# Second feed-forward layer: tiles 4 to 20 as seven products of half blocks instead of eight

## The chip, the cores and the metric

The kernel runs on one core of a Trainium2 chip. The time is device microseconds of one execution; the kernel before was timed three times, and a further execution was recorded by the hardware profiler. The engines in the profile are PE (matrix products; PEld loads its stationary operand), DVE (VectorE), ACT (ScalarE), POOL (GpSimd) and SP (SyncE, which issues nearly all transfers). Each engine works through one queue of instructions in a fixed order, and waits on semaphores for what other engines produce.

## The reference

Two decoder layers on 512 positions of width 1024, in f32: a mixer (gated linear attention in layer 0, latent attention in layer 1), then a feed-forward block. Only the feed-forward block of layer 1 is changed:

```python
def swiglu(h, w_in, w_out):
    gate, up = jnp.split(h @ w_in, 2, axis=-1)
    return (jax.nn.silu(gate) * up) @ w_out
...
        h = modulate(x, norm_ffn[i], sh2, sc2)
        x = x + g2[:, None, :] * swiglu(h, ffn_w_in[i], ffn_w_out[i])
```

`w_in` is 1024 x 5632 (gate and up, 2816 columns each), `w_out` is 2816 x 1024. The 2816 inner columns are 22 tiles of 128.

## The kernel before

Activations are kept transposed: 128 features on the partitions, 512 positions along the free axis. `h` is eight such k-tiles. Every f32 operand of a product is split into a high part (a cast to fp32r on ScalarE) and a low part (the difference, on VectorE), and every product is three matmuls: high x high, high x low, low x high (`mm3`, L175 to L180).

A weight comes as a **unit**, a block of up to 128 x 1024 (`wunit`, L155 to L173): a load from memory into a buffer `raw` (L158, issued by SP), the cast to `wh` (L164, ScalarE), the low part `wl` (L172, VectorE). `raw`, `wh` and `wl` have three buffers each (pool `wp`), so that a load waits until the low part of the unit three loads back is done.

The first two inner tiles are computed in `boundary`, together with the norm ahead of the block, as 256-wide products `fg` (`group`). Tiles 2 to 21 each take two units (gate and up, 512 KB) and `proj` of 8 k-tiles by 3 matmuls of 512 columns for each; then `glu` takes silu (ScalarE), multiplies (VectorE) and splits the result into `acth` and `actl`.

The **output projection** goes over chunks of tiles, so that finished ones can be consumed: after tile 7 over tiles 0 to 7, after tile 14 over 8 to 14, and over 15 to 21 at the end, in the last `boundary`/`finish`. For each of the 8 output k-tiles, `out_proj` (L307) loads one unit of `nk` x 128 columns, multiplies, and adds the product to the residual `x` on VectorE (L290):

```python
        for n in range(KD):
            w = wunit(src[n], nk * P)
            ps = bank("op")
            proj(ps, w, rhs)
            residual(ps, n, l, j, None)
```

The order of the instructions on each engine is set by a scheduler, except on PE inside `manual_schedule`, where the written order holds. Product banks (PSUM) come from two pools of four, `bank` and `abank`; scratch tiles of 128 x 512 come from a ring (`R`).

Of the kernel before, what the change touches and what calls it, by code (L numbers as in the profile page):

```python
# [9 lines left out]
F32 = mybir.dt.float32  # L10
F32R = mybir.dt.float32r
# [3 lines left out]
ALU = mybir.AluOpType  # L15
# [22 lines left out]

DFF = 2816
NFF = DFF // P  # L40
FF_CHUNKS = ((0, 8), (8, 15), (15, 22))

LEVELS = (1, 2, 4, 8, 16, 32, 64)
QB = 32
# [39 lines left out]
def trunk(ctx: ExitStack, tc: tile.TileContext, t: dict, out: bass.AP):  # L84
# [11 lines left out]
    def R(name, dt=F32, cols=S):  # L96
        return ring.tile([P, cols], dt, tag="ring", name=name, bufs=NRING)

    def bank(name):
        return psm.tile([P, S], F32, tag="mm", name=name)  # L100
# [71 lines left out]
        ins = nc.vector.tensor_tensor(out=wl[:, :n], in0=raw[:, :n], in1=wh[:, :n].bitcast(F32), op=ALU.subtract)  # L172
        last["w"] = ins.ins  # L173

    def mm3(ps, a, b, start, stop):  # L175

        (ah, al), (bh, bl) = a, b
        nc.tensor.matmul(ps, lhsT=ah, rhs=bh, start=start, stop=False)  # L178
        nc.tensor.matmul(ps, lhsT=ah, rhs=bl, start=False, stop=False)  # L179
        nc.tensor.matmul(ps, lhsT=al, rhs=bh, start=False, stop=stop)  # L180

    def sl(pair, *idx):
        return pair[0][idx], pair[1][idx]
# [86 lines left out]
                nc.scalar.activation(out=self.acc[:, c], in_=src, func=AF.Square)  # L270
                self.begun |= set(range(c.start, c.stop, P))

    def modulated(hk, k, l, j, rstd, c=FULL):

        hi, lo = hk
        u = R("u")
        nc.vector.scalar_tensor_tensor(out=u[:, c], in0=x[k][:, c], scalar=gs_t[l][j][:, k:k + 1], in1=rstd[:, c],  # L277
                                       op0=ALU.mult, op1=ALU.mult)
        sh = mod[l][3 * j][:, k:k + 1]
        nc.scalar.activation(out=hi[:, c], in_=u[:, c], func=AF.Identity, bias=sh)  # L280
        ins = nc.vector.scalar_tensor_tensor(out=lo[:, c], in0=u[:, c], scalar=sh, in1=hi[:, c].bitcast(F32),
                                             op0=ALU.add, op1=ALU.subtract)
        last["m"] = ins.ins

    def h_tiles():
        return [(R("hh", F32R), R("hl", F32R)) for _ in range(KD)]
# [25 lines left out]
            proj(ps, w, rhs)  # L312
            residual(ps, n, l, j, None)

    def boundary(src, rhs, l, j, nk, name, also=None, grp=None, gl_=None, gj=None, take=None):

        ss = SumSq()
        A, B = HALVES  # L320
        nf = KD - NH
        gw = []
        for n in range(nf):
# [19 lines left out]
        h = h_tiles()  # L343

        def half(n, c):

            ps = bank("op") if c is A else abank("op")
            proj(ps, ws[n - nf], rhs, c=c)
            residual(ps, n, l, j, ss, c)

        def group(c, ps, ks):
            for k in ks:
                if (c.start, k) not in done:
                    modulated(h[k], k, gl_, gj, rstd, c)
                if c.start and k == 3:
                    last["half"] = last["m"]
                for i in range(4):
                    mm3(ps[i][:, c], sl(gw[k], slice(None), slice(i * P, (i + 1) * P)), sl(h[k], slice(None), c),
                        k == 0, k == KD - 1)

        done = set()
        with tc.manual_schedule(engines={mybir.EngineType.PE}):
            for n in range(nf, KD):
                half(n, A)
            half(nf, B)
            ya = rstd_stats(ss.acc, D, name, A)
            half(nf + 1, B)
            rstd_spread(ya, rstd, name, A)
            with tc.high_priority():
                for k in range(2):  # L370
                    modulated(h[k], k, gl_, gj, rstd, A)
# [12 lines left out]
            take(B, pb)  # L384
        return h
# [505 lines left out]
    def ffn(l, prev):  # L891
# [15 lines left out]
            glu(0, ps[0], ps[1], c)  # L907
            glu(1, ps[2], ps[3], c)

        h = prev(grp=t["ffn_s"][l * 4:(l + 1) * 4], gl_=l, gj=1, take=take)  # L910
        for ci, (a, b) in enumerate(FF_CHUNKS):
            for i in range(max(a, 2), b):
                pr = []
                for gu in range(2):
                    with tc.issue_after(last["half"]):
                        w = wunit(t["ffn_in"][l * 40 + (i - 2) * 2 + gu])
                    ps = bank("f")
                    proj(ps, w, h)
                    pr.append(ps)
                ins = glu(i, *pr)  # L920
                if l == 0:
                    with tc.issue_after(ins.ins):
                        more_ada(3)
            src, rhs = t[f"ffn_o{ci}"][l * KD:(l + 1) * KD], [act[i] for i in range(a, b)]
            if l == 0 and ci == 1:
                with tc.issue_after(ins.ins):
                    rotary()
            if ci < 2:
                out_proj(src, rhs, l, 1, nk=b - a)
        return lambda **kw: boundary(src, rhs, l, 1, b - a, f"nf{l}", **kw)  # L930

    nxt = ffn(0, lambda **kw: boundary(t["gla_wo"], oh, 0, 0, KD, "nm0", also=also, **kw))

# [236 lines left out]
def _pack(inp):  # L1170
# [71 lines left out]

    fi = f("ffn_w_in")
    fo = f("ffn_w_out")
    s_, u_, o_ = [], [], [[], [], []]
    for l in range(2):
        g_, up = fi[l][:, :DFF], fi[l][:, DFF:]
        s_.append(pairs(np.concatenate([g_[:, :P], up[:, :P], g_[:, P:2 * P], up[:, P:2 * P]], axis=1)))
        both = np.stack([outer(g_), outer(up)], axis=1)[2:]
        u_.append(both.reshape(40, P, D))  # L1250
        for ci, (a, b) in enumerate(FF_CHUNKS):
            o_[ci].append(outer(fo[l][a * P:b * P]))
    d["ffn_s"] = np.concatenate(s_)
    d["ffn_in"] = np.concatenate(u_)
    for ci in range(3):
        d[f"ffn_o{ci}"] = np.concatenate(o_[ci])

    mw = f("mla_w_in")[0]
    cq, ckv, kr = np.split(mw, [QR, QR + KVR], axis=1)
# [34 lines left out]
```

## Time and profile before

| what | value |
|---|---|
| median of 3 runs | 1181.49 us (1181.05 to 1186.13) |
| profiled execution | 1182.71 us, span 1180.9 us, mean granted clock 0.993 |
| PE busy | 1157.6 us (98%), 7070 instructions |
| VectorE, ScalarE busy | 724.2 us (61%), 417.0 us (35%) |
| second feed-forward layer, tiles 2 to 21 and two projections | 830.90 to 1130.13 us |
| last projection and final norm | 1130.13 to 1180.9 us |

The page's first part gives each engine's busy time and share of the span. Its fourth part follows the chain of work that ended last back from the end; the shares there say which engine set the time. The table of stretches gives, for a window of the span, each engine's busy time with the number of its instructions, then the granted PE clock (1.00 is full), the busy share of the transfer engines, and GB/s. A row of the timeline gives start, duration, engine, line, operation, output and inputs, and in brackets how long the engine had been idle and what ended that. Matmul ends are modelled: the pace of PE is read from the distance of starts.

### The profile page before, as it was taken

The page shows a single profiled execution, that of the slowest core. Times are in us where ns is not written, and L with a number is a line of the kernel's source. Part 1 is how long each engine was busy: PE and PEld are TensorE (multiplying, and loading weights), DVE is VectorE, ACT ScalarE, POOL GpSimd, SP SyncE. Part 2 cuts the span into 40 slices and gives each one's busy share as a digit, 9 for nine tenths or more (in the row PEclk, how much of TensorE's full clock was granted, in tenths as well). Part 3 has the DMA queues.
Part 4 walks back from the last instruction along what each step waited for, and adds up shares of the span by engine and source line. Part 5 has one row for each costly group of instructions (what it writes and reads, how often), then busy time and mean ns, then how long its engine had stood idle before and what let it go on. Part 6 is the DMA issues. An engine that isn't in the chain of part 4 may idle for free.

```text
span 1180.9 us, 17487 instructions
## 1 busy us (share of the span) xinstructions
PE 1157.6 (98%) x7070; PEld 977.4 (83%) x7070; DVE 724.2 (61%) x1428; ACT 417.0 (35%) x666; POOL 18.1 (2%) x40
## 2 busy tenths in 40 slices
PE   8999999999999999999999899999999999999996
PEld 4877878898888888888899788889888888888886
DVE  6987888875663567657566878757324333333345
ACT  3372445342221222222344456534222132222331
POOL 0000000000000000000000022000000000000000
PEclk9999999999999999999999999999999999999998
DMA  9761264714773577366521124140333323233222
GB/s 347 243 188 65 75 230 126 224 62 126 234 246 107 162 242 247 110 204 226 159 85 48 60 81 108 53 126 14 96 106 90 104 93 90 90 107 106 83 78 72
DMA packets 47378, 156.91 MB, mean 133 GB/s; under 512 B 5601, under 2 KB 8033, under 8 KB 47298
## 3 DMA queue, kind: packets, MB, share of 16 engines
q1 hardware_dynamic: 44322, 152.43, 40.5%
q0 software_dynamic: 1536, 2.10, 0.8%
q10 hardware_dynamic: 1440, 1.28, 0.3%
q8 instruction: 55, 0.90, 0.3%
q14 instruction: 25, 0.20, 0.1%
HBM read 151.59 MB, written 2.10 MB: 130 GB/s over the span
## 4 chain that ended last, share of the span: by engine, by line
PE 90%; DVE 7%; DMA 2%; ACT 1%; issue 1%; POOL 0%; SPq 0%; DVEq 0%; ACTq 0%
PE f L179 12%; PE f L178 12%; PE f L180 12%; PE op L178 9%; PE op L179 9%; PE op L180 9%; PE fg L179 2%; PE fg L178 2%; PE fg L180 2%; DMA adaw<-in_ada 1%; PE r L178 1%; PE r L179 1%; PE r L180 1%; PE v L178 1%; DVE wl L172 1%; PE ko L179 1%
## 5 line engine op out<-in xcount | busy, mean ns | idle before, releaser
L164 ACT CAST wh<-raw 128x1024 fp32r<-128x1024 f32 (+2 forms) x173 | 177.4, 1026 | 553.1 <-PE f L179 179.1
L172 DVE TENSOR_TENSOR wl<-raw,wh 128x1024 fp32r<-128x1024 f32 (+2 forms) x181 | 215.2, 1190 | 107.7 <-ACT wh L164 102.0
L179 PE MATMUL f<-hl,wh 128*128 128x512 f32 x640 | 249.1, 389 | 0.0
L178 PE MATMUL f<-hh,wh 128*128 128x512 f32 x640 | 249.1, 389 | 0.0
L180 PE MATMUL f<-hh,wl 128*128 128x512 f32 x640 | 249.0, 389 | 0.0
L178 PE MATMUL op<-acth,wh 128*128 128x512 f32 (+1 forms) x394 | 144.7, 367 | 0.0
L179 PE MATMUL op<-actl,wh 128*128 128x512 f32 (+1 forms) x394 | 144.4, 366 | 0.0
L180 PE MATMUL op<-acth,wl 128*128 128x512 f32 (+1 forms) x394 | 144.4, 366 | 0.0
L180 PEld LDWEIGHTS f<-hh,wl 128*128 128x128 f32 x640 | 120.1, 188 | 25.0
L178 PEld LDWEIGHTS f<-hh,wh 128*128 128x128 f32 x640 | 120.1, 188 | 24.9
L179 PEld LDWEIGHTS f<-hl,wh 128*128 128x128 f32 x640 | 120.1, 188 | 24.8
L290 DVE SCALAR_TENSOR_TENSOR x<-op,mod,x 128x512 f32<-128x512 f32 (+1 forms) x76 | 50.6, 665 | 124.7 <-PE op L180 124.5
L132 DVE SCALAR_TENSOR_TENSOR junk<-adaw,cact 128x1024 bf16<-128x1024 f32 x94 | 114.6, 1219 | 13.4 <-DMA adaw<-in_ada 13.1
L901 DVE TENSOR_TENSOR sg<-sg,f 128x512 f32<-128x512 f32 x40 | 27.5, 687 | 122.8 <-PE f L180 122.8
L178 PEld LDWEIGHTS op<-acth,wh 128*128 128x128 f32 x394 | 74.3, 189 | 12.2
L179 PEld LDWEIGHTS op<-actl,wh 128*128 128x128 f32 x394 | 74.3, 189 | 12.2
L180 PEld LDWEIGHTS op<-acth,wl 128*128 128x128 f32 x394 | 74.3, 189 | 12.1
L280 ACT ACTIVATE hh<-u,mod 128x256 fp32r<-128x256 f32 (+1 forms) x49 | 23.5, 509 | 30.4 <-DVE u L277 30.4
L268 DVE TENSOR_TENSOR acc<-acc,sq 128x512 f32<-128x512 f32 (+1 forms) x45 | 25.1, 557 | 14.6 <-ACT sq L267 14.6
L267 ACT ACTIVATE sq<-x 128x256 f32<-128x256 f32 (+1 forms) x38 | 19.2, 505 | 39.0 <-DVE x L290 38.9
L903 DVE TENSOR_TENSOR actl<-sg,acth 128x512 fp32r<-128x512 f32 (+1 forms) x48 | 30.7, 640 | 0.8 <-ACT acth L902 0.5
L902 ACT CAST acth<-sg 128x512 fp32r<-128x512 f32 (+1 forms) x48 | 28.1, 585 | 7.0 <-DVE sg L901 6.8
(324 smaller groups left out, 1898.0 us busy)
## 6 DMA issues: line engine op xcount, KB each, us to landing
adaw<-in_ada SPq DMA_DIRECT2D x96, 512.0 KB, 4.5
raw<-in_ffn_in SPq DMA_DIRECT2D x80, 512.0 KB, 3.6
raw<-in_ffn_o SPq DMA_DIRECT2D x32, 448.0 KB, 3.3
raw<-in_ffn_o SPq DMA_DIRECT2D x16, 512.0 KB, 3.8
raw<-in_gla_ko SPq DMA_DIRECT2D x8, 512.0 KB, 4.9
raw<-in_gla_v SPq DMA_DIRECT2D x8, 512.0 KB, 4.3
raw<-in_gla_r SPq DMA_DIRECT2D x8, 512.0 KB, 4.1
raw<-in_gla_wo SPq DMA_DIRECT2D x8, 512.0 KB, 3.7
```

The lines of the kernel that those rows point to most:

```text
L132: nc.vector.scalar_tensor_tensor(out=junk, in0=w, scalar=1.0, in1=cact, op0=ALU.mult, op1=ALU.mult, accum_out=acc)
L164: nc.scalar.copy(out=wh[:, :n], in_=raw[:, :n])
L172: ins = nc.vector.tensor_tensor(out=wl[:, :n], in0=raw[:, :n], in1=wh[:, :n].bitcast(F32), op=ALU.subtract)
L178: nc.tensor.matmul(ps, lhsT=ah, rhs=bh, start=start, stop=False)
L179: nc.tensor.matmul(ps, lhsT=ah, rhs=bl, start=False, stop=False)
L180: nc.tensor.matmul(ps, lhsT=al, rhs=bh, start=False, stop=stop)
L268: nc.vector.tensor_tensor(out=self.acc[:, c], in0=self.acc[:, c], in1=sq[:, c], op=ALU.add)
L280: nc.scalar.activation(out=hi[:, c], in_=u[:, c], func=AF.Identity, bias=sh)
L290: ins = nc.vector.scalar_tensor_tensor(out=x[k][:, c], in0=ps[:, c], scalar=mod[l][2 + 3 * j][:, k:k + 1], in1=x[k][:, c], op0=ALU.mult, o ...
L901: ins = nc.vector.tensor_tensor(out=sg[:, c], in0=sg[:, c], in1=pu[:, c], op=ALU.mult)
L902: nc.scalar.copy(out=hi[:, c], in_=sg[:, c])
L903: nc.vector.tensor_tensor(out=lo[:, c], in0=sg[:, c], in1=hi[:, c].bitcast(F32), op=ALU.subtract)
```

## The change

In layer 1 the tiles 4 to 20 are computed in another way. Seen as 2 x 2 blocks, a tile is [gate, up] from two halves of the weights' rows (k-tiles 0 to 3, 4 to 7) and two halves of the positions (A and B, 256 each): eight block products of 4 k-tiles by 256 columns. The new code forms seven products with sums of blocks (a scheme of the Strassen and Winograd kind): P1 to P7, each 4 k-tiles x 3 matmuls of 256 columns.

- `sums` forms, from the kept activations, T1 and T2 for each of four pairs of k-tiles (on VectorE, then split). For that `modulated` keeps its sixteen halves by a further copy on ScalarE.
- `prep` loads both units of a tile (512 KB each), splits the first into `x`, and forms four sums of weights (`sa`, `sb`) on VectorE. `split_y` and `split_w` split the sums `y`, `z` and `w`; the second half of the second unit (`r2`) is split last, in `split_w`.
- `first` has P1 and P2, `second` P3 and P4, `third` P5, `fourth` P6 and P7. P3, P5 and P6 accumulate into the bank of P1, and P7 into that of P4; between them, ScalarE copies the bank out (L1030, L1037, L1045).
- The products are written in this order on PE: P3, P4 of tile i; an output projection if i is 6, 11 or 16; P5 of i; P1, P2 of i + 1; P6, P7 of i.
- The output projection now has four chunks: tiles 0 to 5, 6 to 10, 11 to 15, and 16 to 21 at the end. `out_proj` itself is the same (`wunit` is at L158, its low part at L174, the residual at L294).

Tiles 2, 3 and 21 (`standard`) and all of layer 0 are computed as before.

```diff
-FF_CHUNKS = ((0, 8), (8, 15), (15, 22))
+
+FF_CHUNKS = (((0, 8), (8, 15), (15, 22)), ((0, 6), (6, 11), (11, 16), (16, 22)))
+QUAD0 = 4
...
-    def modulated(hk, k, l, j, rstd, c=FULL):
+    def modulated(hk, k, l, j, rstd, c=FULL, keep=None):
 
         hi, lo = hk
-        u = R("u")
+        u = R("u") if keep is None else keep[k]
...
+        if keep is not None:
+            nc.scalar.activation(out=u[:, c], in_=u[:, c], func=AF.Identity, bias=sh)
...
+        def standard(i, between=None):
+            pr = []
+            for gu in range(2):
+                with tc.issue_after(last["half"]):
+                    w = load(i, gu)
+                ps = bank("f")
+                proj(ps, w, h)
+                if gu == 0 and between is not None:
+                    between()
+                pr.append(ps)
+            return glu(i, *pr)
+
...
+        A, B = HALVES
+        Q = S // 2
+        lo_, hi_ = slice(0, Q), slice(Q, S)
+        KH = KD // 2
+        T = []
+
+        def sums(kp):
+
+            g, g4 = keep[kp], keep[kp + KH]
+            o = []
+            t1, t2 = R("t1"), R("t2")
+            nc.vector.tensor_tensor(out=t1[:, lo_], in0=g[:, A], in1=g[:, B], op=ALU.subtract)
+            nc.vector.tensor_tensor(out=t1[:, hi_], in0=g4[:, B], in1=g[:, B], op=ALU.subtract)
+            nc.vector.scalar_tensor_tensor(out=t2[:, lo_], in0=t1[:, lo_], scalar=-1.0, in1=g4[:, B],
+                                           op0=ALU.mult, op1=ALU.subtract)
+            nc.vector.scalar_tensor_tensor(out=t2[:, hi_], in0=t2[:, lo_], scalar=-1.0, in1=g4[:, A],
+                                           op0=ALU.mult, op1=ALU.subtract)
+            T.append((split(t1, "T1"), split(t2, "T2")))
+
+        def prod(ps, w, wc0, rhs, c, start):
+            for kk in range(KH):
+                wc = slice(wc0 + kk * P, wc0 + (kk + 1) * P)
+                mm3(ps[:, :Q], sl(w, slice(None), wc), sl(rhs(kk), slice(None), c), start and kk == 0,
+                    kk == KH - 1, True)
+
+        def halves2(dst, dc, src, sc):
+
+            hi, lo = dst[0][:, dc], dst[1][:, dc]
+            nc.scalar.copy(out=hi, in_=src[:, sc])
+            nc.vector.tensor_tensor(out=lo, in0=src[:, sc], in1=hi.bitcast(F32), op=ALU.subtract)
+
+        def pair():
+            return (wp.tile([P, 1024], F32R, tag="wh", name="qh"), wp.tile([P, 1024], F32R, tag="wl", name="ql"))
+
+        L, U = slice(0, S), slice(S, 2 * S)
+        qd = {}
+
+        def prep(i):
+
+            r1, r2 = [wp.tile([P, 1024], F32, tag="raw", name=f"q{n}") for n in range(2)]
+            for gu, r in enumerate((r1, r2)):
+                nc.sync.dma_start(out=r, in_=t["ffn_in"][l * 40 + (i - 2) * 2 + gu])
+            x_ = pair()
+            nc.scalar.copy(out=x_[0], in_=r1)
+            sa = att.tile([P, 1664], F32, tag="ah", name="sa")
+            sb = att.tile([P, 1664], F32, tag="al", name="sb")
+            nc.vector.tensor_tensor(out=x_[1], in0=r1, in1=x_[0].bitcast(F32), op=ALU.subtract)
+            nc.vector.tensor_tensor(out=sb[:, L], in0=r2[:, L], in1=r2[:, U], op=ALU.add)
+            nc.vector.tensor_tensor(out=sa[:, U], in0=r1[:, L], in1=r2[:, L], op=ALU.add)
+            nc.vector.tensor_tensor(out=sa[:, L], in0=r1[:, L], in1=sb[:, L], op=ALU.add)
+            nc.vector.tensor_tensor(out=sb[:, U], in0=r1[:, U], in1=sa[:, L], op=ALU.add)
+            qd[i] = dict(x=x_, r2=r2, sa=sa, sb=sb)
+
+        def split_y(i):
+            d = qd[i]
+            d["y"] = pair()
+            halves2(d["y"], slice(0, 1024), d["sa"], slice(0, 1024))
+            z = ap_.tile([P, D], F32R, tag="adaw", name="qz")
+            d["z"] = (z[:, L], z[:, U])
+            halves2(d["z"], L, d["sb"], L)
+
+        def split_w(i):
+            d = qd[i]
+            d["w"] = pair()
+            halves2(d["w"], L, d["sb"], U)
+            halves2(d["w"], U, d["r2"], U)
+
+        hk = lambda off: (lambda kk: h[kk + off])
+        Tk = lambda j: (lambda kk: T[kk][j])
+
+        def first(i):
+            d = qd[i]
+            d["a"], d["b"], d["d"] = bank("f"), bank("f"), abank("f")
+            d["sn"], d["su"] = R("sn"), R("su")
+            prod(d["a"], d["x"], 0, hk(0), A, True)
+            nc.scalar.copy(out=d["sn"][:, lo_], in_=d["a"][:, :Q])
+            prod(d["b"], d["x"], S, hk(KH), A, True)
+            nc.vector.tensor_tensor(out=d["su"][:, hi_], in0=d["sn"][:, lo_], in1=d["b"][:, :Q], op=ALU.add)
+
+        def second(i):
+            d = qd[i]
+            prod(d["a"], d["y"], 0, Tk(1), lo_, False)
+            nc.scalar.copy(out=d["sn"][:, hi_], in_=d["a"][:, :Q])
+            prod(d["d"], d["y"], S, Tk(0), hi_, True)
+            d["sg"] = R("sg")
+            nc.scalar.activation(out=d["sg"][:, lo_], in_=d["su"][:, hi_], func=AF.Silu)
+
+        def third(i):
+            d = qd[i]
+            prod(d["a"], d["z"], 0, Tk(0), lo_, False)
+            nc.scalar.copy(out=d["su"][:, lo_], in_=d["a"][:, :Q])
+            d["cn"] = R("cn")
+            nc.vector.tensor_tensor(out=d["cn"][:, hi_], in0=d["su"][:, lo_], in1=d["d"][:, :Q], op=ALU.add)
+
+        def fourth(i):
+            d = qd.pop(i)
+            prod(d["a"], d["w"], 0, hk(KH), B, False)
+            nc.scalar.activation(out=d["sg"][:, hi_], in_=d["a"][:, :Q], func=AF.Silu)
+            prod(d["d"], d["w"], S, Tk(1), hi_, False)
+            nc.vector.tensor_tensor(out=d["cn"][:, lo_], in0=d["sn"][:, hi_], in1=d["d"][:, :Q], op=ALU.add)
+            act[i] = hi, lo = R("acth", F32R), R("actl", F32R)
+            nc.vector.scalar_tensor_tensor(out=d["cn"], in0=d["sg"], scalar=-1.0, in1=d["cn"],
+                                           op0=ALU.mult, op1=ALU.mult)
+            nc.scalar.copy(out=hi, in_=d["cn"])
+            nc.vector.tensor_tensor(out=lo, in0=d["cn"], in1=hi.bitcast(F32), op=ALU.subtract)
+
+        quads = range(QUAD0, NFF - 1)
+        with tc.manual_schedule(engines={mybir.EngineType.PE}):
+            for i in range(2, QUAD0):
+                standard(i)
+                for kp in range(2):
+                    sums((i - 2) * 2 + kp)
+            prep(quads[0])
+            first(quads[0])
+            split_y(quads[0])
+            for i in quads:
+                last_ = i == quads[-1]
+                if not last_:
+                    prep(i + 1)
+                second(i)
+                for ci in range(1, len(chunks)):
+                    if i == chunks[ci][0]:
+                        src, rhs, nk = out_args(ci - 1)
+                        out_proj(src, rhs, l, 1, nk=nk)
+                third(i)
+                split_w(i)
+                if last_:
+                    standard(i + 1, lambda: fourth(i))
+                else:
+                    first(i + 1)
+                    split_y(i + 1)
+                    fourth(i)
+        src, rhs, nk = out_args(len(chunks) - 1)
```

The order of the instructions moves with it. First, VectorE around the first output projection of layer 1. Rows give line, operation, output and inputs; `wl` are the low parts of the weight units, `op` the products of the projection (the n-th unit's `wl` and `op` have numbers that differ by 3), `x0`, `x1`, `x2` the residual. Before:

```order
L172 TENSOR_TENSOR wl_8954<-raw_8951,wh_8953 128x1024
L903 TENSOR_TENSOR actl_8876<-sg_8877,acth_8875 128x512
L172 TENSOR_TENSOR wl_8986<-raw_8983,wh_8985 128x1024
L901 TENSOR_TENSOR sg_8946<-sg_8946,f_8919 128x512
L172 TENSOR_TENSOR wl_9018<-raw_9015,wh_9017 128x1024
L903 TENSOR_TENSOR actl_8945<-sg_8946,acth_8944 128x512
L290 SCALAR_TENSOR_TENSOR x0_80<-op_8957,mod1_5_106,x0_80 128x512
L172 TENSOR_TENSOR wl_9050<-raw_9047,wh_9049 128x1024
L290 SCALAR_TENSOR_TENSOR x1_81<-op_8989,mod1_5_106,x1_81 128x512
L172 TENSOR_TENSOR wl_9082<-raw_9079,wh_9081 128x1024
L290 SCALAR_TENSOR_TENSOR x2_82<-op_9021,mod1_5_106,x2_82 128x512
```

Now:

```order
L1059 TENSOR_TENSOR actl_9051<-cn_8978,acth_9050 128x512
L174 TENSOR_TENSOR wl_9099<-raw_9096,wh_9098 128x768
L294 SCALAR_TENSOR_TENSOR x0_80<-op_9102,mod1_5_106,x0_80 128x512
L174 TENSOR_TENSOR wl_9125<-raw_9122,wh_9124 128x768
L294 SCALAR_TENSOR_TENSOR x1_81<-op_9128,mod1_5_106,x1_81 128x512
L174 TENSOR_TENSOR wl_9151<-raw_9148,wh_9150 128x768
L294 SCALAR_TENSOR_TENSOR x2_82<-op_9154,mod1_5_106,x2_82 128x512
L174 TENSOR_TENSOR wl_9177<-raw_9174,wh_9176 128x768
```

Before, the low part of the third unit (`wl_9018`) stands ahead of the first residual, and that of the fourth right behind it; now the low part of the second unit (`wl_9125`) stands behind the first residual, and so on.

Second, ScalarE at the tiles 2 to 4, from the cast of tile 2's activations. `T1h` and `T2h` are high parts of activation sums, `qh` of weight sums. Before:

```order
L902 CAST acth_8599<-sg_8601 128x512
L164 CAST wh_8708<-raw_8706 128x1024
L900 ACTIVATE sg_8670<-f_8612 128x512
L164 CAST wh_8746<-raw_8744 128x1024
L902 CAST acth_8668<-sg_8670 128x512
L164 CAST wh_8777<-raw_8775 128x1024
L900 ACTIVATE sg_8739<-f_8681 128x512
L164 CAST wh_8815<-raw_8813 128x1024
```

Now, from the cast of tile 3's activations:

```order
L908 CAST acth_8706<-sg_8708 128x512
L983 CAST qh_8849<-sb_8749 128x512
L983 CAST qh_8849<-q1_8742 128x512
L201 CAST T1h_8719<-t1_8713 128x512
L201 CAST T2h_8723<-t2_8714 128x512
L201 CAST T1h_8733<-t1_8727 128x512
L201 CAST T2h_8737<-t2_8728 128x512
L1030 COPY sn_8758<-f_8755 128x256
L1040 ACTIVATE sg_8832<-su_8759 128x256
L1037 COPY sn_8758<-f_8755 128x256
```

Where a cast of weights and the silu of the next tile stood, there are now the casts of the last two pairs of sums, and behind them the copy of the bank of P1 of tile 4 (L1030).

More of the change, by code (lines that the diff above doesn't have):

```diff
@@ L343, in boundary @@
         h = h_tiles()
+        if keep is not None:
+            keep += [R("u") for _ in range(KD)]
         def half(n, c):
@@ L370, in boundary @@
                 for k in range(2):
-                    modulated(h[k], k, gl_, gj, rstd, A)
+                    modulated(h[k], k, gl_, gj, rstd, A, keep)
                     done.add((A.start, k))
@@ L908, in take @@
             glu(1, ps[2], ps[3], c)
[L910 to L921, printed above, removed]
+        keep = [] if l == 1 else None
@@ new lines, in ffn, with load, out_args @@
+        h = prev(grp=t["ffn_s"][l * 4:(l + 1) * 4], gl_=l, gj=1, take=take, keep=keep)
+        chunks = FF_CHUNKS[l]
+        def load(i, gu):
+            return wunit(t["ffn_in"][l * 40 + (i - 2) * 2 + gu])
+        def out_args(ci):
+            a, b = chunks[ci]
+            return t[f"ffn_o{l}{ci}"], [act[i] for i in range(a, b)], b - a
+        def standard(i, between=None):
[9 more added lines that the diff above has]
+            return glu(i, *pr)
@@ L922, in ffn @@
+        if l == 0:
+            for ci, (a, b) in enumerate(chunks):
+                for i in range(max(a, 2), b):
+                    ins = standard(i)
                     with tc.issue_after(ins.ins):
                         more_ada(3)
[L924 to L929, printed above, removed]
@@ L1244, in _pack @@
     fo = f("ffn_w_out")
-    s_, u_, o_ = [], [], [[], [], []]
+    s_, u_ = [], []
     for l in range(2):
```

27 lines of the change are left out of this document (16 added, 11 removed).

## The prediction

> **What bounds the kernel now.** I read the page's busy table and its chain of waits first, then the table of stretches for the second feed-forward layer, then single rows. The page:
>
> ```profile
> PE 1157.6 (98%) x7070; PEld 977.4 (83%) x7070; DVE 724.2 (61%) x1428; ACT 417.0 (35%) x666; POOL 18.1 (2%) x40
> PE 90%; DVE 7%; DMA 2%; ACT 1%; issue 1%; POOL 0%; SPq 0%; DVEq 0%; ACTq 0%
> ```
>
> The matmul engine (PE) is busy 98% of the span and carries 90% of the chain. An average may hide stages, so the stretches come next (busy us and instructions of PE, weight load, VectorE, ScalarE, GpSimd; then clock, DMA share, GB/s):
>
> ```profile
> 840.00:900.00 60.00, 60.00 (x266) 49.71 (x265) 21.21 (x23) 17.33 (x22) 0.00 (x0) 1.00 0.32 98
> 900.00:950.00 50.00, 50.00 (x222) 41.39 (x222) 17.04 (x17) 10.00 (x10) 0.00 (x0) 1.00 0.35 101
> 1174.00:1180.90 6.90, 0.93 (x4) 0.64 (x3) 3.71 (x10) 0.00 (x0) 0.00 (x0) 0.50 0.55 191
> ```
>
> In the changed layer PE never pauses, at full clock, while VectorE (DVE) has 21 of 60 us. So a matmul taken away is time won, as long as its replacement keeps PE fed; and a wait of 1 us that reaches PE is 1 us lost.
>
> **What the products save.** PE's own rows give the two paces (start, modelled duration, line, operands):
>
> ```profile
> 825.74 0.28 PE L180 MATMUL fg<-hh,gwl 128*128 128x256 f32 x1
> ...
> 830.78 0.28 PE L180 MATMUL fg<-hh,gwl 128*128 128x256 f32 x1
> 830.90 0.40 PE L178 MATMUL f<-hh,wh 128*128 128x512 f32 x1
> ```
>
> ```profile
> 1130.13 0.39 PE L178 MATMUL op<-acth,wh 128*128 128x512 f32 x1
> ...
> 1151.21 0.39 PE L178 MATMUL op<-acth,wh 128*128 128x512 f32 x1
> ```
>
> From 825.74 to 830.78 lie 42 steps of 256 columns: 0.120 us each, weights loaded anew for every one. From 1130.13 to 1151.21 lie 93 steps of 512: 0.2267 us. A tile is 2 x 8 x 3 = 48 matmuls of 512 columns, 10.88 us; as seven products it is 84 of 256, 10.08 us (1.44 per product). So 0.80 us a tile, not an eighth: half as wide, a matmul costs 0.53 of the wide one. Times 17 tiles: **-13.6 us**. [...]
>
> **What the output projection adds.** It now runs at tiles 6, 11 and 16, between products P4 and P5, with units of 6, 5 and 5 k-tiles. At that place two of the three raw buffers hold the second halves of tiles i and i+1, which are split later. So one buffer circulates: a unit's load waits for the low part (wl) of the unit before. And VectorE's queue now reads wl0, x0, wl1, x1: wl of unit n+1 stands behind the residual x of unit n, which waits for that unit's last matmul. PE's third matmul of unit n+1 needs that wl. Before, wl ran two or three units ahead of x. The rows:
>
> ```profile
> 917.74 0.39 PE L180 MATMUL op<-acth,wl 128*128 128x512 f32 x1
> 917.97 0.39 PE L178 MATMUL op<-acth,wh 128*128 128x512 f32 x1
> 918.17 0.75 DVE L290 SCALAR_TENSOR_TENSOR x<-op,mod,x 128x512 f32<-128x512 f32 x1 [3.35 <-PE op L180]
> ```
>
> ```profile
> 842.08 0.69 DVE L901 TENSOR_TENSOR sg<-sg,f 128x512 f32<-128x512 f32 x1 [3.42 <-PE f L180]
> 842.87 1.22 DVE L172 TENSOR_TENSOR wl<-raw,wh 128x1024 fp32r<-128x1024 f32 x1
> 844.01 0.68 DVE L903 TENSOR_TENSOR actl<-sg,acth 128x512 fp32r<-128x512 f32 x1
> 844.12 0.33 SPq L158 DMA_DIRECT2D raw<-in_ffn_in  x1
> ```
>
> The next unit's first matmul (917.97) does not wait for x; x starts 0.04 us after the modelled end 917.74 + 0.39. Back-to-back VectorE work overlaps by 0.08 (844.01 - 842.87 = 1.14 for an operation of 1.22), and a load goes out 0.03 after the wl that frees its buffer. Durations by shape, VectorE (L172 to L290) and ScalarE (L164 to L900):
>
> ```profile
> L172 DVE TENSOR_TENSOR wl<-raw,wh 128x1024 fp32r<-128x1024 f32 x44 | 53.9, 1225 | 66.3 <-ACT wh L164 63.0
> L903 DVE TENSOR_TENSOR actl<-sg,acth 128x512 fp32r<-128x512 f32 x19 | 13.0, 683 | 0.0
> L172 DVE TENSOR_TENSOR wl<-raw,wh 128x896 fp32r<-128x896 f32 x10 | 10.9, 1092 | 7.7 <-ACT wh L164 7.5
> ```
>
> ```profile
> L164 ACT CAST wh<-raw 128x1024 fp32r<-128x1024 f32 x44 | 46.4, 1055 | 174.5 <-PE f L179 78.1 <-issue 50.7 <-PE op L179 45.7
> L902 ACT CAST acth<-sg 128x512 fp32r<-128x512 f32 x19 | 11.8, 621 | 0.1
> L164 ACT CAST wh<-raw 128x896 fp32r<-128x896 f32 x10 | 9.5, 948 | 37.9 <-PE op L179 18.4 <-issue 11.8 <-PE f L179 7.7
> ```
>
> 128 columns cost VectorE 0.133 and ScalarE 0.107 us, so wl is 0.96 us at 768 and 0.83 at 640 columns, the cast 0.84 and 0.73. From the start of unit n's last matmul to the third of n+1: 0.39 + 0.04 + 0.75 - 0.08 + 0.96 + 0.04 = 2.10 us (1.97 with 5 k-tiles), where PE alone needs three steps, 0.68. That is 1.42 and 1.29 us lost at each of seven steps between units: 9.9 + 9.0 + 9.0 = **+27.9 us**. A unit takes 18 x 0.2267 + 1.42 = 5.50 us instead of 4.08, or 4.69 instead of 3.40. The loads:
>
> ```profile
> raw<-in_ffn_in SPq DMA_DIRECT2D x37, 512.0 KB, 3.6
> raw<-in_ffn_o SPq DMA_DIRECT2D x16, 448.0 KB, 3.2
> out<-y SPq DMA_DIRECT2D x2, 128.0 KB, 1.7
> DMA to landing us min/median/max: 3.0/3.6/5.4
> ```
>
> Between 128 and 512 KB a line gives 2.97 us for 384 and 2.65 for 320 KB. The loop wl, load, cast, wl is then 0.03 + 2.97 + 0.04 + 0.84 + 0.04 + 0.96 = 4.88, shorter than 5.50, so x, not the load, decides. Were x out of the way, this loop would still cost 0.80 and about 0.9 a step: +18, the lower bound. The upper: the slowest landing seen, 1.8 over the median, at half of the 21 steps, less the 0.62 that the loop has spare: +12 more.
>
> The **first unit** of each projection: its load waits until the first half of tile i+1 is split. That split ends about 2.85 us after P2 of tile i (sums of weights for 1.7 us, 1.14 for the split), then load, cast and wl take 4.9; PE, after P6, P7, P3, P4 and two matmuls, is there at 6.2. So +1.6 at tile 6. At 11 and 16 the smaller unit gives 1.0, and about 1.1 of lateness from the tile loop below adds to it: 2.1 each. **+5.9 us**.
>
> **The start.** VectorE gets four pairs of activation sums (16 sums of 256 columns, 8 splits of 512) and the weight sums and splits of tiles 4 and 5. The queue orders show them after tile 2's second projection (842.08 above) as a block without a free slot: until the last sum, 3 operations of 1024, 17 of 512, 16 of 256. The 256-wide rows stand in the boundary:
>
> ```profile
> L277 DVE SCALAR_TENSOR_TENSOR u<-x,gs,rstd 128x256 f32<-128x256 f32 x16 | 7.2, 478 | 0.0
> L268 DVE TENSOR_TENSOR acc<-acc,sq 128x256 f32<-128x256 f32 x6 | 2.5, 423 | 2.3 <-ACT sq L267 2.3
> L249 ACT COPY rstd<-nm_bc 128x256 f32<-128x256 f32 x2 | 0.7, 351 | 0.0
> ```
>
> Overlapped: 3 x 1.14 + 17 x 0.60 + 16 x 0.38 = 19.7 us; at full durations 22.5. PE is done with tiles 2 and 3 and with P1, P2 of tile 4 at 830.90 + 96 x 0.2267 + 2.88 = 855.5. On ScalarE the copy of P1 out of its bank (L1030) stands behind the last cast of the sums (T2h), and P3 may not write that bank before the copy. So P3 starts at 842.1 + 19.7 + 0.62 + 0.35 + some 0.1 = 862.8, or 865.6 with full durations. I take 863.7, since blocks that hand over between engines overlap only in part: **+8.2 us**, bounds 7 and 10. [...]
>
> **The steady tile.** VectorE has two operations of 1024 columns, nine of 512 (four sums, three splits, the product and its low part) and three of 256: 2.28 + 5.4 + 1.14 = 8.8 us overlapped, 9.9 at full durations, against 10.08 on PE. ScalarE has 2 x 1.055 + 4 x 0.62 + 5 x 0.35 = 6.3; P5 and P6 wait there for copies of the bank that they add to, 0.35 each with a product of 1.44 between, which fits. The load loop: the buffer of a second half is freed, 3.6 to land, then until the next is freed sums 2.4, x and y splits 2.28, two additions 0.76, w splits 1.2: 10.3 us, 0.2 a tile too long. Between projections are at most five tiles, 1.1 us, and P6 comes 2.8 us after the chain of its w splits would be done (P6 starts 7.2 us after P3, and what VectorE and ScalarE do until w is split takes 4.4). So PE sees **0**; with a 5.4 landing each time the loop is 12.1.
>
> On SyncE's queue the loads of tile i+2 now stand behind the projection's eight. They are needed eight products, 11.5 us, after it, and take 3.6 + 1.06 + 1.22 = 5.9 to load and split: hidden. The sixteen copies that keep the modulated activations (ScalarE, 0.35 to 0.5 each) come in the boundary:
>
> ```profile
> 800.00:826.00 26.00, 25.86 (x237) 25.32 (x227) 20.77 (x62) 13.49 (x26) 0.00 (x0) 1.00 0.04 8
> ```
>
> There ScalarE is idle half the time and PE full: 0; without that cover half of 16 x 0.35, +3. The last chunk has 6 k-tiles, not 7, so that its first unit is loaded and split 0.1 to 0.2 earlier: -0.1.
>
> **Sum**: -13.6 + 27.9 + 5.9 + 8.2 - 0.1 = +28.3. The profiled run is 1182.71, so 1211.0; it lies 1.2 above the median of 1181.49, so the forecast is **1210 us**.
>
> **Rivals.** (A) This forecast, 1195 to 1225, 0.72. (B) Faster: wl is early enough. It would be so if x waited for nothing, which needs unit steps on PE of at most 4.1 and 3.4 us; then the products' 13.6 stays, less up to 8 at the start: 1168 to 1176. For it speaks that VectorE is only 61% busy; against it the order of its queue, which idle time does not alter. 0.07. (C) The loop of loads and VectorE bounds each tile at 12.1, not 10.08: ten tiles outside the reach of a projection add 20, so 1230. The slow landings of 5.4 speak for it, the median of 3.6 against. 0.15. (D) The waits cost about half of what I sum and cancel the gain: 0.06. It would take the loop's lower bound and a hidden start: -13.6 + 18 + 0 = +4. That the change does not run fewer columns of matmul is excluded by its rows: 84 x 256 is 7/8 of 48 x 512.
>
> **Range and chances.** A measurement here tells 0.5%, about 6 us, from no change. The range 1192 to 1234 runs from the lower bound of the projections with first units and start at half (-13.6 + 18 + 3 + 4 = +11) to C with two slow landings on top (1.8 each). Faster 0.07, within 0.5% 0.06, slower 0.87.
>
> **What would show it.** Right: PE's steps of 0.120 in the products and 10.08 a tile; in the three projections units of 5.5 and 4.7 us, where PE waits for wl and wl starts when x ends; one pause of about 8 us on PE near 855 to 864; PE still the longest in the busy table, VectorE up by 17 tiles' extra work. Wrong: units at 4.08 and 3.40; a pause ahead of P6 in every tile (then C); 256-wide steps well over 0.120.

## The result: slower by 3.6%

The changed kernel takes 1224.43 us (median of 4, 1220.11 to 1228.02) against 1181.27 us before (median of 4): a ratio of 1.0358, 95% interval 1.0336 to 1.0381. The profiled execution took 1220.11 us, with a span of 1218.3 us.

First the page of the changed kernel, its busy table and its chain:

```profile
PE 1160.0 (95%) x7673; PEld 994.0 (82%) x7673; DVE 828.3 (68%) x1638; ACT 478.6 (39%) x817; POOL 18.0 (1%) x40
PE 77%; DVE 14%; DMA 5%; issue 2%; ACT 1%; SPq 0%; DVEq 0%; ACTq 0%
```

PE's share of the chain falls from 90% to 77%, and that of VectorE doubles to 14%, though it is busy only 68% of the time. So PE now waits for VectorE at places, not on average. PE's busy time even rose by 2.4 us where 13.6 us of products were saved: a matmul at half clock, or held up behind a wait, counts as busy for longer (0.63 and 0.50 us in rows below, instead of 0.39). The stretches say where (the first is the start at tile 4, the next two are the projections at tiles 6 and 11, the last the five tiles between the projections at 6 and 11):

```profile
853.50:860.40 6.90, 0.05 (x1) 0.00 (x0) 6.82 (x16) 3.78 (x7) 0.00 (x0) 0.74 0.25 80
884.00:935.00 51.00, 40.39 (x154) 29.09 (x153) 14.92 (x19) 8.99 (x13) 0.00 (x0) 0.93 0.25 75
986.00:1025.00 39.00, 31.80 (x122) 21.60 (x123) 12.94 (x18) 7.14 (x12) 0.00 (x0) 1.00 0.26 74
935.15:986.00 50.85, 50.55 (x421) 50.34 (x419) 43.95 (x69) 29.21 (x53) 0.00 (x0) 1.00 0.30 97
```

The tiles keep PE full: 50.55 us busy of 50.85. In the projections it is busy 40 of 51 and 32 of 39 us, with VectorE at a third: nobody is short of throughput there. At the start PE stands still for 6.9 us while VectorE works through. The last matmul of P2, and the rows that end the pause:

```profile
853.27 0.28 PE L182 MATMUL f<-hh,ql 128*128 128x256 f32 x1
...
859.52 0.62 ACT L201 CAST T2h<-t 128x512 fp32r<-128x512 f32 x1 [0.60 <-DVE t L970]
860.04 0.37 ACT L1030 COPY sn<-f 128x256 f32<-128x256 f32 x1
860.46 0.58 PE L180 MATMUL f<-T2h,qh 128*128 128x256 f32 x1 [6.92 <-ACT sn L1030]
```

The cast of the last T2 waits for VectorE's last sum (L970), the copy of P1's bank stands behind that cast, and P3 starts 0.05 us after the copy ends.

To compare traces I use the **layer time**: from the first full-width matmul of tile 2 to the first of the last projection. In the kernel before it is 299.23 us; with the new chunks 5.44 us of output products lie inside it that came later before, so the reference is 304.67. The changed kernel's is 343.70, +39.0. By segments of PE's rows, measured less the matmuls' own pace:

| part | us |
|---|---|
| products, 17 tiles of 10.08 instead of 10.88 | -13.6 |
| start at tile 4: a pause of 7.3, then 1.2 of half clock | +8.5 |
| wait ahead of the first unit, tiles 6, 11, 16: 2.0, 1.6, 1.6 | +5.2 |
| inside the three projections: 15.5, 10.5, 12.9 | +38.9 |
| sum | +39.0 |

The changed layer starts 2.2 us earlier in this execution (828.73 against 830.90), and what follows it takes 0.5 us more, so the spans differ by 37.4 only. In the profiled executions of all kernels below, that start lies between 826.4 and 831.4; the layer time leaves it out.

One step between units in the second projection, all engines:

```profile
995.69 0.39 PE L182 MATMUL op<-acth,wl 128*128 128x512 f32 x1
995.82 0.73 ACT L166 CAST wh<-raw 128x640 fp32r<-128x640 f32 x1 [4.00 <-DMA raw<-in_ffn_o]
996.11 0.75 DVE L294 SCALAR_TENSOR_TENSOR x<-op,mod,x 128x512 f32<-128x512 f32 x1 [3.31 <-PE op L182]
996.60 0.50 PE L180 MATMUL op<-acth,wh 128*128 128x512 f32 x1 [0.52 <-ACT wh L166]
996.78 0.81 DVE L174 TENSOR_TENSOR wl<-raw,wh 128x640 fp32r<-128x640 f32 x1
997.65 0.50 PE L182 MATMUL op<-acth,wl 128*128 128x512 f32 x1 [0.32 <-DVE wl L174]
```

The last matmul of a unit starts at 995.69 and, with its modelled 0.39, ends at 996.08; the residual x starts 0.03 later; wl of the next unit starts as x ends, and PE's third matmul at 997.65, when wl is there. That is 1.96 us from the last matmul to the third, where 1.97 was worked out. The trace adds what the forecast left out: the cast arrives late as well (its load had just landed), so part of the wait shows ahead of the first matmul, yet x and wl still end the step.

### The profile page after: what moved, and what is told of

It is laid out like the page before. It is cut to its first block, busy times and chain, and to the rows that moved or that the text cites. A ratio compares the mean times of both kernels' runs of the same rounds, so it can differ in the third digit from the quotient of the medians.

```text
span 1218.3 us, 19090 instructions
## 1 busy us (share of the span) xinstructions
PE 1160.0 (95%) x7673; PEld 994.0 (82%) x7673; DVE 828.3 (68%) x1638; ACT 478.6 (39%) x817; POOL 18.0 (1%) x40
## 3 DMA queue, kind: packets, MB, share of 16 engines
q10 hardware_dynamic: 1440, 1.28, 0.3%
## 4 chain that ended last, share of the span: by engine, by line
PE 77%; DVE 14%; DMA 5%; issue 2%; ACT 1%; SPq 0%; DVEq 0%; ACTq 0%
PE op L182 9%; PE f L180 9%; PE f L181 9%; PE f L182 9%; PE op L180 9%; PE op L181 8%; DVE wl L174 3%; DMA q<-in_ffn_in 2%; PE fg L181 2%; PE fg L180 2%; PE fg L182 2%; PE v L180 1%; DMA raw<-in_ffn_o 1%; PE v L182 1%; PE v L181 1%
## 5 line engine op out<-in xcount | busy, mean ns | idle before, releaser
L166 ACT CAST wh<-raw 128x1024 fp32r<-128x1024 f32 (+3 forms) x147 | 143.0, 973 | 437.9 <-PE op L181 101.4
L174 DVE TENSOR_TENSOR wl<-raw,wh 128x1024 fp32r<-128x1024 f32 (+3 forms) x155 | 174.7, 1128 | 39.6 <-ACT wh L166 37.8
L294 DVE SCALAR_TENSOR_TENSOR x<-op,mod,x 128x512 f32<-128x512 f32 (+1 forms) x84 | 56.5, 673 | 158.6 <-PE op L182 158.3
L180 PE MATMUL f<-hh,wh 128*128 128x512 f32 x368 | 143.2, 389 | 0.0
L181 PE MATMUL f<-hl,wh 128*128 128x512 f32 x368 | 143.2, 389 | 0.0
L182 PE MATMUL f<-hh,wl 128*128 128x512 f32 x368 | 143.2, 389 | 0.0
L134 DVE SCALAR_TENSOR_TENSOR junk<-adaw,cact 128x1024 bf16<-128x1024 f32 x94 | 114.6, 1220 | 10.5 <-DMA adaw<-in_ada 10.5
L180 PEld LDWEIGHTS f<-hh,wh 128*128 128x128 f32 x368 | 69.1, 188 | 14.3
L182 PEld LDWEIGHTS f<-hh,wl 128*128 128x128 f32 x368 | 69.1, 188 | 14.3
L907 DVE TENSOR_TENSOR sg<-sg,f 128x512 f32<-128x512 f32 x23 | 15.8, 687 | 64.2 <-PE f L182 64.2
L181 PE MATMUL f<-hl,qh 128*128 128x256 f32 x204 | 57.7, 283 | 0.0
L182 PE MATMUL f<-hh,ql 128*128 128x256 f32 x204 | 57.7, 283 | 0.0
L180 PE MATMUL f<-hh,qh 128*128 128x256 f32 x204 | 57.7, 283 | 0.0
```

The source lines that it names most:

```text
L134: nc.vector.scalar_tensor_tensor(out=junk, in0=w, scalar=1.0, in1=cact, op0=ALU.mult, op1=ALU.mult, accum_out=acc)
L166: nc.scalar.copy(out=wh[:, :n], in_=raw[:, :n])
L294: ins = nc.vector.scalar_tensor_tensor(out=x[k][:, c], in0=ps[:, c], scalar=mod[l][2 + 3 * j][:, k:k + 1], in1=x[k][:, c], op0=ALU.mult, o ...
L907: ins = nc.vector.tensor_tensor(out=sg[:, c], in0=sg[:, c], in1=pu[:, c], op=ALU.mult)
```

## The experiments

Two questions were open. In the projections: is it the one circulating buffer, the order of VectorE's queue, or the short chunks? At the start: is it VectorE's block of sums, or the place of one copy? All kernels of one group were timed with the kernel before on the same chip.

**Only the four chunks.**

```diff
-        if l == 0:
+        if True:
             for ci, (a, b) in enumerate(chunks):
                 for i in range(max(a, 2), b):
                     ins = standard(i)
...
-        keep = [] if l == 1 else None
+        keep = None
```

> All tiles of layer 1 by the eight half products as before (48 matmuls of 512 columns), no kept activations and no sums; only the output projection goes over the four new chunks. Theory (the loss comes from what circulates beside the seven products): the same matmuls in another order, raw buffers all free for the units, low parts two units ahead of the residuals, so 1181, within 4 us of the kernel before. Rival (a projection over 5 or 6 k-tiles is itself too short to load its units under): a unit of 5 k-tiles is 3.40 us on PE against 2.65 + 0.73 + 0.83 to load and split it; if that pair could not overlap, each of the 24 units would lose 0.8, so 1200.

1181.57 us, ratio 0.9997 (0.9982 to 1.0012). Layer time 304.67, to the last digit the reference, so PE never pauses. Short units are harmless when all three raw buffers circulate and the low parts run ahead of the residuals.

**A fourth raw buffer.**

```diff
-    NRING = 54
+    NRING = 52
...
-        raw = wp.tile([P, 1024], F32, tag="raw", name="raw")
+        raw = wp.tile([P, 1024], F32, tag="raw", name="raw", bufs=4)
...
-            r1, r2 = [wp.tile([P, 1024], F32, tag="raw", name=f"q{n}") for n in range(2)]
+            r1, r2 = [wp.tile([P, 1024], F32, tag="raw", name=f"q{n}", bufs=4) for n in range(2)]
```

> The changed kernel with a fourth raw buffer (the ring of scratch tiles has 52 instead of 54 to pay for it). Two buffers now circulate in a projection, and the queue of VectorE puts the low part of the next unit ahead of the residual. Theory: PE's waits inside the three projections (38.9 us in the changed kernel's trace, half clock included) and ahead of their first units (5.2) nearly vanish, 40 of 44 us; the start's pause of 7.3 stays: 1224 - 40 = 1184, between 1178 and 1190. Rival (the loads and VectorE bound the steady tiles too): a buffer more only moves the wait, tiles stretch beyond 10.08, and it ends over 1200.

1179.23 us, ratio 0.998 (0.9966 to 0.9995). Two projections and the five tiles between them, as stretches:

```profile
889.29:921.95 32.66, 32.66 (x146) 27.03 (x145) 14.50 (x21) 7.04 (x10) 0.00 (x0) 1.00 0.38 112
921.95:972.35 50.40, 50.40 (x422) 50.39 (x421) 43.46 (x67) 30.06 (x54) 0.00 (x0) 1.00 0.29 94
972.35:999.57 27.22, 27.22 (x122) 22.53 (x121) 12.92 (x19) 6.29 (x10) 0.00 (x0) 1.00 0.40 113
```

PE is full in all of them: 32.66 us for 144 matmuls of 512 columns (32.64 by pace), 27.22 for 120 (27.20). So all waits of the projections and of their first units, 44 us, go with the fourth buffer. The five tiles take 50.40, or 10.08 each, and VectorE has 43.46 / 5 = 8.7 us of work per tile, so the rival of a bound in the steady tile falls.

But the fourth buffer also changed the order: the scheduler now puts wl of the next unit ahead of x. On VectorE, in the first projection:

```profile
890.28 0.96 DVE L174 TENSOR_TENSOR wl<-raw,wh 128x768 fp32r<-128x768 f32 x1 [0.98 <-ACT wh L166]
893.60 0.75 DVE L294 SCALAR_TENSOR_TENSOR x<-op,mod,x 128x512 f32<-128x512 f32 x1 [2.36 <-PE op L182]
894.26 0.95 DVE L174 TENSOR_TENSOR wl<-raw,wh 128x768 fp32r<-128x768 f32 x1
```

The first row is wl of the second unit (that of the first started at 887.74), the second the residual of the first unit, the third wl of the third unit. The next two kernels take buffer and order apart.

**Three buffers, wl of the next unit ahead of x.**

```diff
+        w = wunit(src[0], nk * P)
         for n in range(KD):
-            w = wunit(src[n], nk * P)
             ps = bank("op")
             proj(ps, w, rhs)
-            residual(ps, n, l, j, None)
+            if l == 1 and n + 1 < KD:
+                w = wunit(src[n + 1], nk * P)
+                with tc.issue_after(last["w"]):
+                    residual(ps, n, l, j, None)
+            else:
...
```

> The changed kernel with three raw buffers, but on VectorE the low part of unit n+1 is queued ahead of the residual of unit n. Theory (order of the queue and one circulating buffer, each with its own bound): what is left is the loop low part, load, cast, low part, 4.9 us a unit at 6 k-tiles and 4.5 at 5 (with the landing of 2.9 us that the changed kernel's trace shows), instead of 5.6 and 4.8 there; over 7 and 14 steps that gives back 5 + 4 = 9 us: 1215. Rival A (the order of the queue is the whole cause): all of some 28 us come back, 1196. Rival B (the circulating buffer is the whole cause): 1224, no change.

**Four buffers, wl of the next unit behind x.**

```diff
+        ins = None
         for n in range(KD):
-            w = wunit(src[n], nk * P)
+            w = wunit(src[n], nk * P, split_=False)
+            if l == 1 and ins is not None:
+                with tc.issue_after(ins.ins):
+                    wunit_lo(w, nk * P)
+            else:
+                wunit_lo(w, nk * P)
             ps = bank("op")
-            proj(ps, w, rhs)
-            residual(ps, n, l, j, None)
+            proj(ps, w[:2], rhs)
+            ins = residual(ps, n, l, j, None)
```

> Four raw buffers as above, but on VectorE the low part of unit n+1 is held behind the residual of unit n, as in the changed kernel. Theory (the order of the queue is a sufficient cause by itself): 1.29 to 1.42 us and a slower first step after each pause remain at each of 21 steps, 28 to 31 us, only the wait ahead of the first units (5.2) and late loads go: 1216, between 1210 and 1221. Rival (the buffer is the cause and the order only follows it): as with four buffers alone, 1184.

The first took 1212.31 us, ratio 1.0261 (1.0214 to 1.0309); the second 1210.12 us, 1.0239 (1.0213 to 1.0264). Layer times 334.24 and 331.48. Neither the order alone nor the buffer alone gives back more than about a third. With the order changed and one buffer, VectorE waits for the cast and PE for both:

```profile
991.12 0.72 ACT L166 CAST wh<-raw 128x640 fp32r<-128x640 f32 x1 [3.95 <-PE op L181]
991.88 0.83 DVE L174 TENSOR_TENSOR wl<-raw,wh 128x640 fp32r<-128x640 f32 x1 [3.18 <-ACT wh L166]
991.90 0.50 PE L180 MATMUL op<-acth,wh 128*128 128x512 f32 x1 [0.57 <-ACT wh L166]
992.73 0.33 SPq L160 DMA_DIRECT2D raw<-in_ffn_o  x1
...
995.79 0.72 ACT L166 CAST wh<-raw 128x640 fp32r<-128x640 f32 x1 [3.94 <-PE op L181]
```

wl ends at 992.71, the next load goes out at 992.73, and the next cast starts 3.06 after that. It takes 0.72, then PE starts again: 4.67 us a unit (991.90 to 996.57) where PE needs 3.40. (The cast's bracket names a matmul whose modelled end falls at that moment. The loads of this projection landed 2.8 to 3.1 us after their issue, and this cast starts 3.06 after the issue of its own; for other units of these projections the bracket names the load.) With two circulating buffers and the old order, the load is no longer in it:

```profile
988.29 0.39 PE L182 MATMUL op<-acth,wl 128*128 128x512 f32 x1
988.52 0.39 PE L180 MATMUL op<-acth,wh 128*128 128x512 f32 x1
988.72 0.75 DVE L294 SCALAR_TENSOR_TENSOR x<-op,mod,x 128x512 f32<-128x512 f32 x1 [3.38 <-PE op L182]
988.75 0.39 PE L181 MATMUL op<-actl,wh 128*128 128x512 f32 x1
989.38 0.82 DVE L174 TENSOR_TENSOR wl<-raw,wh 128x640 fp32r<-128x640 f32 x1
990.26 0.51 PE L182 MATMUL op<-acth,wl 128*128 128x512 f32 x1 [1.12 <-DVE wl L174]
990.60 0.40 PE L180 MATMUL op<-acth,wh 128*128 128x512 f32 x1
```

The first two matmuls go on at once and the third waits: from 988.75 to 990.26 is 1.51 us, 1.28 over the pace. It repeats 14 times with 1.28 or 1.29, and at 6 k-tiles 7 times with 1.42: the two sizes worked out in the forecast, to 0.01. The step after the wait takes 0.34 instead of 0.23, and with such slow first steps a projection loses 11.0, 10.2 and 10.2 us, 31.4 in all. In the three projections of the kernel with the order alone it is 8.9, 9.2 and 10.2, so 28.2. Two locks, then: with either one closed 28 to 31 us remain, and none with both open.

**Without the sums of activations.** (P3, P4, P5 and P7 take plain k-tiles of h in their place; the sums and their splits are left out.)

```diff
-                for kp in range(2):
-                    sums((i - 2) * 2 + kp)
+        T.extend((h[kk], h[kk + KH]) for kk in range(KH))
```

> Four raw buffers, and the sums of activations with their splits left out (products P3, P4, P5 and P7 take plain k-tiles of h in their place, so the output is another one; all matmuls stay). Theory (the block of sums on VectorE makes the start late): it is 16 x 0.38 + 8 x 0.60 = 10.9 us, more than PE's pause of 7.3 us before P3 of tile 4, so the pause and the half clock after it (2.5 us in the trace with four buffers) both go: 1179 - 10 = 1169, between 1167 and 1171. Rival (the weight sums of tiles 4 and 5, or their loads, are late anyway): most of the pause stays, 1176 or more.

1169.03 us, ratio 0.988 (0.9844 to 0.9916). No pause, no half clock in the layer; its time is 291.17, 13.50 under the reference. That is the saving of the products, undisturbed. (The weight sums of all tiles are still in it, so by themselves they do not make the start late.)

**Seven products from tile 5, from tile 6, and the copy ahead of the last sums.** All three have four raw buffers.

```diff
-QUAD0 = 4
+QUAD0 = 5
...
-                for kp in range(2):
+                for kp in range(2) if i < 4 else ():
                     sums((i - 2) * 2 + kp)
```

> Four raw buffers, and the seven products begin at tile 5 instead of 4: one tile more by the eight half products (0.80 us), under which the sums have 10.9 us more of PE's time. Theory: the pause of 7.3 and its half clock of 2.5 go, 0.8 comes: 1179 - 9 = 1170, between 1168 and 1172. Rival (loads or weight sums hold up the first product tile wherever it lies): the pause moves along with it, 1179 to 1180.

```diff
-QUAD0 = 4
+QUAD0 = 6
...
-                for kp in range(2):
-                    sums((i - 2) * 2 + kp)
+                sums(i - 2)
```

> Four raw buffers, the seven products begin at tile 6, one pair of sums behind each of the tiles 2 to 5. Theory: no pause either, but 0.8 us a tile less gained: 1171, 0.8 above the start at tile 5. Rival (at tile 6 the first product tile meets the first projection, whose units then wait for the loads of two tiles): a wait of some 5 us ahead of the first unit, 1176.

```diff
-                for kp in range(2):
+                for kp in range(2) if i < 3 else range(1):
                     sums((i - 2) * 2 + kp)
             prep(quads[0])
-            first(quads[0])
+            cp = first(quads[0])
+            with tc.issue_after(cp.ins):
+                sums(3)
```

(`first` returns its copy L1030 as `cp`.)

> Four raw buffers, start at tile 4; the copy of P1's bank on ScalarE is queued ahead of the last pair of sums and their casts, which follow it. Theory (VectorE's block of work decides, the copy's place in the queue only adds itself): P3 could begin about 1 us sooner, but its last k-tile still waits for the last pair; 1178, between 1175 and 1180. Rival (the copy's place is the cause): the pause is gone, 1169.

From tile 5: 1169.98 us, ratio 0.9897 (0.9865 to 0.9929), layer time 291.96, 12.71 under the reference (16 tiles by 0.80 are 12.8). Around the start and over the rest of the tiles and projections:

```profile
852.00:866.00 14.00, 14.00 (x77) 12.17 (x76) 14.00 (x25) 8.27 (x13) 0.00 (x0) 1.00 0.18 61
878.45:1108.00 229.55, 229.55 (x1574) 214.51 (x1573) 160.33 (x242) 104.67 (x179) 0.00 (x0) 1.00 0.33 102
```

VectorE is still full from 852 to 866, but PE has a tile's work meanwhile. After that PE is busy all 229.55 us, at full clock.

From tile 6: 1174.99 us, ratio 0.9946 (0.9925 to 0.9968), and here theory and rival both failed; that the time lies near the rival's 1176 is chance. There is no wait ahead of the first unit, but a pause of 3.3 us ahead of P3 and 2.5 us of half clock after it:

```profile
870.52 0.69 DVE L907 TENSOR_TENSOR sg<-sg,f 128x512 f32<-128x512 f32 x1 [1.73 <-PE f L182]
...
873.10 0.42 DVE L966 TENSOR_TENSOR t<-u 128x256 f32<-128x256 f32 x1
...
876.02 0.37 ACT L1030 COPY sn<-f 128x256 f32<-128x256 f32 x1
```

The last pair of sums (L966) was queued behind tile 5's activation (L907), which waits for tile 5's last matmul; VectorE even idled 1.73 us for it. By these rows, where a block of work stands in the queue matters, not only whether there is time for it; no further run tested that.

With the copy first: 1181.38 us, ratio 0.9984 (0.9962 to 1.0007). The one pause became four, of 3.5, 2.1, 1.0 and 0.3 us beyond the pace, 6.9 in place of 7.6, since P3 now waits for the sums themselves:

```profile
854.56 0.39 PE L180 MATMUL f<-T2h,qh 128*128 128x256 f32 x1 [3.35 <-ACT sn L1030]
...
858.37 0.58 PE L180 MATMUL f<-T2h,qh 128*128 128x256 f32 x1 [1.82 <-ACT T2h L201]
859.52 0.58 PE L181 MATMUL f<-T2l,qh 128*128 128x256 f32 x1 [0.57 <-DVE T2l L202]
```

The half clock is 2.8 us instead of 2.5. Layer time 301.01, against 301.31 with four buffers alone. So the copy's place added about 0.7 of the 7 us of pause; the block of sums is the rest.

## The prediction, point by point

- **PE bounds the layer, and what reaches PE is lost**: right. Where nothing holds it up, PE is at 100% in all stretches.
- **The products, -13.6**: right. 420 matmuls in 50.40 us are 0.1200 each, and without pauses the layer gains 13.50.
- **Steps between units, +27.9**: right in mechanism and in the size of the wait (1.28 and 1.42 measured, 1.29 and 1.42 worked out), short by 11.0 against the 38.9 of the table. Some 1.9 of the 38.9 lies in the first units, ahead of and at their third matmul (0.9, 0.5, 0.5), which the forecast counted under the first units. The steps themselves are short by 9.1, and the term left out three things. The first step after a wait is slower (0.34 us instead of 0.23), so 21 steps cost 31.4 with four buffers and the old order: +3.5. The clock fell to half three times in the projections, 19 matmuls at 0.427 instead of 0.227: +3.8. Two loads landed late, 4.7 and 3.9 us after their issue, where the others took about 2.9, and the steps behind them took 1.0 and 0.7 more than the rest: +1.7. The forecast held late loads only as an upper bound.
- **One lock or two**: the forecast said that x, not the load, decides, and gave +18 for the load's loop alone. With x out of the way the projections still lost 28.2. Of the difference, 2.8 is half clock and some 4 the load, which is the term mis-sized: in the rows above the loop takes 4.66 us (0.02 to the issue, 3.06 to the cast, cast 0.72, 0.03, wl 0.83; the median landing is 3.0), where the forecast had 4.32 with a landing of 2.65, read from the line between 128 and 512 KB. The rest lies mostly in late landings and in the first units. So at 5 k-tiles the two loops lie close together: about 4.8 us a unit in the changed kernel, 4.6 to 4.7 with x out of the way.
- **First units, +5.9**: 5.2 ahead of the first matmul. The forecast reckoned to the third matmul, and with the 1.9 from above it is 7.1.
- **The start, +8.2 (7 to 10)**: right in mechanism, as the rows of the copy show. The pause is 7.3, in range, plus half clock, which the sum does not have: 1.2 here, 2.5 in the kernel with four buffers. P3 starts at 860.46; moved by the 2.2 us of the earlier layer start that is 862.6, the forecast's figure for overlapped operations (862.8), not the 863.7 it took.
- **The steady tile, 0**: right. With four buffers VectorE had 8.7 us a tile (8.8 worked out), ScalarE 6.0 (6.3). Rival C, tiles of 12.1, did not come: in the changed kernel PE was busy 50.55 of 50.85.
- **Rival B, faster**: not here, but its condition (units of at most 4.1 and 3.4 us) is met with a fourth buffer. With that alone the time is 1179, since the start costs 10 and not up to 8; from tile 5 it is 1170, in the rival's range of 1168 to 1176.
- **The total**: 1210 forecast, 1224 measured, range 1192 to 1234. In the recorded execution the layer is 10.7 us above the sum; its other parts balance to -1.6. The remaining 4.3, between that execution and the median, has no trace: the four executions lie 8 us apart, and which of their waits differ stays open. That 1224 lies within the range is in part luck: its upper end was drawn from rival C and slow landings, while most of what was missing came from the half clock and the slower first steps, which the sum did not have.

## What to carry to other kernels

Fewer matmul columns are worth what the rows of PE say (0.80 us a tile here, not an eighth), and only if the buffers that the new scheme holds are not those that the neighbouring stage needs to run ahead. When work holds a buffer across a stage that streams through the same pool, count what is left to circulate, and read in the queue's order whether the next unit's preparation stands behind the last one's result: either alone cost some 30 us here, and one more buffer of 4 KB per partition opened both. Work done once at the start of a pipeline needs matmuls to lie under, and a place in the queue that comes before the wait, not behind it.

## What was not expected of the hardware

The clock fell to half after pauses much shorter than that at the start. Rows of PE in the first projection of the changed kernel:

```profile
906.23 0.50 PE L180 MATMUL op<-acth,wh 128*128 128x512 f32 x1 [1.71 <-ACT wh L166]
906.57 0.39 PE L181 MATMUL op<-actl,wh 128*128 128x512 f32 x1
907.22 0.50 PE L182 MATMUL op<-acth,wl 128*128 128x512 f32 x1 [0.26 <-DVE wl L174]
...
908.08 0.63 PE L182 MATMUL op<-acth,wl 128*128 128x512 f32 x1
908.51 0.63 PE L180 MATMUL op<-acth,wh 128*128 128x512 f32 x1
908.93 0.63 PE L181 MATMUL op<-actl,wh 128*128 128x512 f32 x1
...
911.45 0.40 PE L181 MATMUL op<-actl,wh 128*128 128x512 f32 x1
```

PE had waited 1.7 and then 0.3 us. From 908.08, steps take 0.43 instead of 0.23 us, for some 3.4 us. At the first unit of the third projection, waits of 1.6 and 0.3 us were followed by the same. Yet waits of 1.6 and 0.3 us at the first unit of the second projection were followed by none (the granted clock is 1.00 from 911.38 to 1078.63), nor were the 21 waits of 1.3 to 1.4 us in the kernel with four buffers and the old order (no step of 0.43 us in its projections).

The granted clock was 0.50 for 3.41 us at each of the three places in the projections (from 887.49, 907.97 and 1078.63), and for 6.83 us at the start (from 856.77). Part of that fell into the pause, and 13 matmuls ran at half clock; at the start with four buffers it was 27 (1.2 and 2.5 us lost), so it is not a fixed price. The 3.41 us at half clock of the rows above, with as much ahead and behind (the clock is the third figure from the end):

```profile
904.56:907.97 3.41, 1.48 (x5) 0.95 (x6) 1.71 (x2) 0.83 (x1) 0.00 (x0) 1.00 0.00 0
907.97:911.38 3.41, 3.41 (x9) 2.65 (x9) 0.00 (x0) 0.83 (x1) 0.00 (x0) 0.50 0.41 115
911.38:914.80 3.42, 2.17 (x9) 1.44 (x9) 1.62 (x2) 0.00 (x0) 0.00 (x0) 1.00 0.00 0
```

Both waits fall into the first of these stretches, in which PE is busy 1.48 of 3.41 us. The waits at the second and the third projection are nearly alike (1.64 and 0.29 us, 1.55 and 0.30 beyond the pace), and only the latter were followed by half clock. So the length of the waits alone does not tell when it comes; what does was not shown, and no run was made to test it.

The other surprise is the first step after a wait: at full clock 0.33 to 0.35 us instead of 0.23 for 512 columns, in all the projections with waits.
